# Retention branch: the gate takes the group norm's weight and offset when it is evicted, the norm becomes two operations per head, and POOL does no arithmetic

## The chip, the cores and the metric

The kernel runs on one core of a Trainium2 chip. The metric is the device time of one execution in microseconds (us), the median of several runs. The engines are named as the profile names them: PE (TensorE matmuls), PEld (its weight loads), DVE (VectorE), ACT (ScalarE), POOL (GpSimd), SP (SyncE, which here only issues transfers).

## The reference

One layer of a hybrid decoder: from `h = rms_norm(x)` a wide projection gives an attention branch and a retention branch; both are merged through sigmoid gates, projected back, and followed by a squared-ReLU MLP. 256 positions, model width 2048, 8 retention heads with values of width 256. The part that matters here:

```
rg, rv ...   = h @ w_in                         # gate and values of the retention branch, 2048 columns each
y_ret        = retention_chunkwise(rq, rk, rv)  # (256, 8 heads, 256)
mu, var      = mean and variance of y over the 256 columns of a head
yn           = (y - mu) * rsqrt(var + 1e-6)
o_ret        = silu(rg) * (yn * ret_gn_g + ret_gn_b)
merged       = sigmoid(ga) * (o_attn @ w_up_attn) + sigmoid(gb) * (o_ret @ w_up_ret)
```

## The kernel before

All large products run as three fp32r matmuls of a high and a low part (lines 335 to 337: high x high, high x low, low x high), 128 rows by 512 columns each. Weights are streamed in tiles; ACT copies half a tile into its high part `whi` (line 293), DVE subtracts to get the low part `wlo` (line 294). One such half tile, called a split below, serves two steps of the inner dimension k, that is 12 matmuls. `whi` and `wlo` have three buffers each, so a split is made while the two before it are still to be multiplied.

`run_block` (line 319) multiplies one block of 512 output columns: 16 steps of k, for two row tiles t = 0, 1. In each step it first calls `step()`, which advances every piece of side work in the list `work` by one `yield`; side work is written as generators, and this sets where its instructions stand among the matmuls. `drain()` runs what is left. Within what the program order allows, the compiler's scheduler may still place the instructions of one engine in another order.

The retention part is the loop at line 695, over j = 0..3, two heads at a time. Each round multiplies the gate block RG (512 columns), evicts it as silu (ACT's sigmoid in line 398, DVE's multiplication in line 707), multiplies the value block RV and evicts it. The side work `decayed` (lines 632 to 643) runs during RV of the same round. `retain` and `normed` (lines 645 to 693) run during the next block: RG of round j + 1, or the block GB after the last round. So `normed` of round 0 stands in RG of round 1, and so on.

In `normed`, DVE takes means and variances (lines 677, 678), then a reciprocal square root in eleven tiny operations (lines 346 to 351), then (y - mu) * r in line 688. POOL multiplies by the weight (line 690), adds the offset (line 691) and multiplies by the gate (line 692), 512 columns each, for t = 0 and then t = 1. Seven steps of k after each was issued, PE transposes the result (line 368, a helper). The transposes of t = 0 stand before step 14 of the block and those of t = 1 before step 15, the last one. PE takes its instructions in order, so a transpose that waits holds back all matmuls behind it.

The tiles `mid` come from a ring of 11 buffers. Before, a round takes 6 of them: weight and offset `gb[0]`, `gb[1]` (loaded over POOL's queue, line 699), two gates, two value tiles.

Of the kernel before, what the change touches and what calls it, by code (L numbers as in the profile page):

```python
# [14 lines left out]
ALU = mybir.AluOpType  # L15
AX = mybir.AxisListType

P = 128
# [4 lines left out]
BN = 512  # L23
# [7 lines left out]
RV = 256  # L31
# [106 lines left out]
def block_kernel(ctx, tc, cst, rot, xt, gains, w, x, ret_gn_g, ret_gn_b, out):  # L138
    nc = tc.nc
# [21 lines left out]
    def nm(s):  # L161
        uid[0] += 1
        return f"{s}_{uid[0]}"

    def stage(shape=(P, BN)):
        return sp.tile(list(shape), F32, tag="stg", name=nm("stg"), bufs=n_stg)

    def mid(shape):
        return ep.tile(list(shape), F32, tag="mid", name=nm("mid"), bufs=n_mid)

    def small(w):
        return sp.tile([P, w], F32, tag="small", name=nm("small"), bufs=n_sm)
# [4 lines left out]
    def psum_a():  # L177
        return pa.tile([P, BN], F32, tag="pa", name=nm("pa"))
# [5 lines left out]
    work = []  # L184
# [6 lines left out]
    def drain():  # L191
        while work:
            step()
# [125 lines left out]
    def run_block(key, act, before=None):  # L319
        nk, n = B[key]  # L320
        ps = [pm.tile([P, BN], F32, tag="pm", name=nm("pm")) for _ in range(T)]
        for k in range(nk):
            if k % HC == 0:
                ws = weights((key, k // KC, k % KC // HC))
            if before:
                before(k)
            step()
            products(ps, [p[:, :n] for p in (ws[0][:, k % HC], ws[1][:, k % HC])], [act(k, t) for t in range(T)], k == 0, k == nk - 1)
        return [p[:, :n] for p in ps]
# [9 lines left out]
    def of(a):  # L339
        return lambda k, t: tuple(z[:, k, t * P:(t + 1) * P] for z in a[:2])  # L340


    def rsqrt(v, n, mul):

        a, y, u = small(n), small(n), small(n)
        nc.vector.tensor_scalar(a, v, mul, EPS, op0=ALU.mult, op1=ALU.add)
        nc.vector.tensor_scalar(y.bitcast(I32), a.bitcast(I32), -0.5, float(0x5F3759DF), op0=ALU.mult, op1=ALU.add)
        for _ in range(3):
            nc.vector.tensor_tensor(u, y, y, op=ALU.mult)
            nc.vector.scalar_tensor_tensor(u, u, -0.5, a, op0=ALU.mult, op1=ALU.mult)  # L350
            nc.vector.scalar_tensor_tensor(y, u, 1.5, y, op0=ALU.add, op1=ALU.mult)
        return y
# [9 lines left out]
    def transpose_in(act, k0, t, src, wait=2):  # L362

        for _ in range(wait):
            yield
        ps = psum_t()
        for c in range(4):
            nc.tensor.transpose(ps[:, c * P:(c + 1) * P], src[:, c * P:(c + 1) * P], ident)  # L368
        split_into(act, k0, 4, t, ps)
# [27 lines left out]
    def evict(dst, ps, t, func=AF.Copy):  # L397
        nc.scalar.activation(dst, ps, func, scale=r1[:, t:t + 1])
# [233 lines left out]
    def decayed(j, am):  # L632
        h0 = 2 * j
        yield
        psA = psum_a()
        for a in range(2):
            for t in range(T):
                nc.tensor.matmul(psA[:, (2 * a + t) * P:(2 * a + t + 1) * P], rkT[:, h0 + a, t * P:(t + 1) * P],
                                 rqT[:, h0 + a, t * P:(t + 1) * P], start=True, stop=True)
        for a in range(2):  # L640
            nc.vector.tensor_tensor(am[:, a * S:(a + 1) * S].rearrange("p (t i) -> p t i", t=T),
                                    psA[:, a * S:(a + 1) * S].rearrange("p (t i) -> p t i", t=T),
                                    dec[:, h0 + a].unsqueeze(1).to_broadcast([P, T, P]), op=ALU.mult)

    def retain(j, silu, rv, gb, am):
        h0 = 2 * j
        psR = psum_a()
        for a in range(2):
            nc.tensor.matmul(psR[:, a * RV:(a + 1) * RV], kz[:, h0 + a, :], rv[0][:, a * RV:(a + 1) * RV], start=True, stop=True)
        R = stage()  # L650
        nc.scalar.activation(R, psR, AF.Copy)
        yield
        ys = []
        for t in range(T):
            psy = psum_a()
            for a in range(2):
                nc.tensor.matmul(psy[:, a * RV:(a + 1) * RV], am[:, (2 * a + t) * P:(2 * a + t + 1) * P],
                                 rv[t][:, a * RV:(a + 1) * RV], start=True, stop=True)
            y = stage()
            nc.scalar.activation(y, psy, AF.Copy)  # L660
            ys.append(y)
            yield
        psc = psum_a()
        for a in range(2):
            nc.tensor.matmul(psc[:, a * RV:(a + 1) * RV], rqT[:, h0 + a, P:S], R[:, a * RV:(a + 1) * RV], start=True, stop=True)
        for a in range(2):
            y = ys[1][:, a * RV:(a + 1) * RV]
            nc.vector.scalar_tensor_tensor(y, psc[:, a * RV:(a + 1) * RV], xi[:, h0 + a:h0 + a + 1], y,
                                           op0=ALU.mult, op1=ALU.add)
        yield from normed(j, ys, silu, gb)  # L670

    def normed(j, ys, silu, gb):
        mv, vr = small(4 * T), small(2 * T)
        for t in range(T):
            for a in range(2):
                st = small(6)
                nc.vector.bn_stats(st, ys[t][:, a * RV:(a + 1) * RV])
                nc.vector.bn_aggr(mv[:, 4 * t + 2 * a:4 * t + 2 * a + 2], st)
        nc.vector.tensor_copy(vr, mv.rearrange("p (a b) -> p a b", b=2)[:, :, 1])
        yield  # L680
        r = rsqrt(vr, 2 * T, 1.0)
        yield
        for t in range(T):
            y = ys[t]
            for a in range(2):
                yy = y[:, a * RV:(a + 1) * RV]
                i = 2 * t + a
                nc.vector.tensor_scalar(yy, yy, mv[:, 2 * i:2 * i + 1], r[:, i:i + 1], op0=ALU.subtract, op1=ALU.mult)
            yield
            nc.gpsimd.tensor_tensor(y, y, gb[0], op=ALU.mult)  # L690
            nc.gpsimd.tensor_tensor(y, y, gb[1], op=ALU.add)  # L691
            nc.gpsimd.tensor_tensor(y, y, silu[t], op=ALU.mult)  # L692
            work.append(transpose_in(rT, 4 * j, t, y, W_GN))

    for j in range(4):
        gb = []
        for src in (ret_gn_g, ret_gn_b):
            g = mid([P, BN])
            nc.gpsimd.dma_start(g, src[:, j * BN:(j + 1) * BN].to_broadcast([P, BN]))
            gb.append(g)  # L700
        ps = run_block(("RG", j), of(hT))
        drain()
        silu = []
        for t in range(T):
            s = mid([P, BN])
            evict(s, ps[t], t, AF.Sigmoid)
            nc.vector.scalar_tensor_tensor(s, ps[t], r1[:, t:t + 1], s, op0=ALU.mult, op1=ALU.mult)
            silu.append(s)
        am = stage()
        work.append(decayed(j, am))  # L710
        ps = run_block(("RV", j), of(hT))
        rv = []
        for t in range(T):
            v = mid([P, BN])
            evict(v, ps[t], t)
            rv.append(v)
        work.append(retain(j, silu, rv, gb, am))


    for i in range(4):  # L720
# [122 lines left out]
    ys = {}  # L843
# [126 lines left out]
```

## Time and profile before

| | before |
|---|---|
| median of 3 runs | 1651.04 us (1648.32 to 1652.44) |
| the profiled execution, its own time | 1649.92 us |
| its span, first to last instruction | 1648.1 us |
| PE busy | 1632.5 us (99%) |
| DVE busy | 1155.4 us (70%) |
| ACT busy | 931.4 us (57%) |
| POOL busy | 103.1 us (6%) |
| mean granted clock of TensorE | 0.999 |

Times in the profile are counted from the start of the span. A matmul's bar overlaps the next one's, because matmuls are pipelined: a 128x512 matmul is shown with 0.39 us, and the next one starts 0.23 us after it.

### The profile page before, as it was taken

The page shows a single profiled execution, that of the slowest core. Times are in us where ns is not written, and L with a number is a line of the kernel's source. Part 1 is how long each engine was busy: PE and PEld are TensorE (multiplying, and loading weights), DVE is VectorE, ACT ScalarE, POOL GpSimd, SP SyncE. Part 2 cuts the span into 40 slices and gives each one's busy share as a digit, 9 for nine tenths or more (in the row PEclk, how much of TensorE's full clock was granted, in tenths as well). Part 3 has the DMA queues.
Part 4 walks back from the last instruction along what each step waited for, and adds up shares of the span by engine and source line. Part 5 has one row for each costly group of instructions (what it writes and reads, how often), then busy time and mean ns, then how long its engine had stood idle before and what let it go on. Part 6 is the DMA issues. An engine that isn't in the chain of part 4 may idle for free.

```text
span 1648.1 us, 19358 instructions
## 1 busy us (share of the span) xinstructions
PE 1632.5 (99%) x7466; PEld 1351.6 (82%) x7466; DVE 1155.4 (70%) x1316; ACT 931.4 (57%) x1150; POOL 103.1 (6%) x92
## 2 busy tenths in 40 slices
PE   9999999999999999999999999999999999999998
PEld 8977888888888778778888888888888888888887
DVE  6577776644554666564555578898989898989874
ACT  7556564444334444434444476676767676767672
POOL 0000000000000330220000000000000000000000
PEclk9999999999999999999999999999999999999999
DMA  9644445555555444445557655777777777767763
GB/s 346 223 144 176 148 149 187 181 191 192 199 186 197 157 171 167 175 171 187 194 188 266 209 209 209 230 230 230 230 229 230 228 228 218 230 221 228 229 196 136
DMA packets 62940, 334.47 MB, mean 203 GB/s; under 512 B 6656, under 2 KB 13184, under 8 KB 27264
## 3 DMA queue, kind: packets, MB, share of 16 engines
q1 hardware_dynamic: 51264, 309.62, 52.3%
q0 software_dynamic: 8704, 16.78, 6.8%
q10 hardware_dynamic: 2880, 6.83, 1.1%
q8 instruction: 58, 0.95, 0.2%
q14 instruction: 34, 0.28, 0.0%
HBM read 314.34 MB, written 18.87 MB: 202 GB/s over the span
## 4 chain that ended last, share of the span: by engine, by line
PE 56%; issue 3%; POOL 1%; DVE 0%; POOLq 0%
PE pf L335 7%; PE pf L337 7%; PE pf L336 7%; PE pm L337 6%; PE pm L335 6%; PE pm L336 6%; PE pq L337 5%; PE pq L335 5%; PE pq L336 5%; PE pt L368 1%; POOL stg L690 0%; PE pt L770 0%; POOL stg L691 0%; POOL stg L692 0%; DVE stg L885 0%
## 5 line engine op out<-in xcount | busy, mean ns | idle before, releaser
L294 DVE TENSOR_TENSOR wlo<-raw,whi 128x1024 fp32r<-128x1024 f32 (+2 forms) x564 | 678.3, 1211 | 411.1 <-ACT whi L293 405.8
L293 ACT ACTIVATE whi<-raw 128x1024 fp32r<-128x1024 f32 (+2 forms) x564 | 581.9, 1037 | 552.3 <-PE pm L337 433.6
L335 PE MATMUL pm<-whi,act 128*128 128x512 f32 (+1 forms) x1312 | 517.3, 395 | 1.7 <-ACT whi L293 1.7
L336 PE MATMUL pm<-wlo,act 128*128 128x512 f32 (+1 forms) x1312 | 507.5, 387 | 0.0
L337 PE MATMUL pm<-whi,act 128*128 128x512 f32 (+1 forms) x1312 | 506.8, 386 | 0.0
L335 PEld LDWEIGHTS pm<-whi,act 128*128 128x128 f32 x1312 | 246.9, 188 | 50.9 <-issue 3.2
L336 PEld LDWEIGHTS pm<-wlo,act 128*128 128x128 f32 x1312 | 247.1, 188 | 48.2 <-issue 1.9
L337 PEld LDWEIGHTS pm<-whi,act 128*128 128x128 f32 x1312 | 246.8, 188 | 47.6
L335 PE MATMUL pf<-whi,act 128*128 128x512 f32 x512 | 200.3, 392 | 0.0
L336 PE MATMUL pf<-wlo,act 128*128 128x512 f32 x512 | 199.6, 390 | 0.0
L337 PE MATMUL pf<-whi,act 128*128 128x512 f32 x512 | 199.6, 390 | 0.0
L294 DVE TENSOR_TENSOR wlo<-rawc,whi 128x1024 fp32r<-128x1024 f32 x112 | 136.8, 1221 | 26.8 <-ACT whi L293 25.6
L335 PE MATMUL pq<-whi,xf 128*128 128x512 f32 x392 | 154.5, 394 | 0.0
L337 PE MATMUL pq<-whi,xf 128*128 128x512 f32 x392 | 152.9, 390 | 0.0
L336 PE MATMUL pq<-wlo,xf 128*128 128x512 f32 x392 | 152.8, 390 | 0.0
L293 ACT ACTIVATE whi<-rawc 128x1024 fp32r<-128x1024 f32 x112 | 118.7, 1059 | 47.3 <-PE pf L337 23.3
L286 DVE TENSOR_TENSOR raw<-raw,raw 128x2048 f32<-128x2048 f32 x56 | 128.0, 2286 | 0.5
L337 PEld LDWEIGHTS pf<-whi,act 128*128 128x128 f32 x512 | 96.1, 188 | 20.0
L335 PEld LDWEIGHTS pf<-whi,act 128*128 128x128 f32 x512 | 96.1, 188 | 20.0 <-ACT whi L293 0.4
L336 PEld LDWEIGHTS pf<-wlo,act 128*128 128x128 f32 x512 | 96.2, 188 | 19.8
L882 POOL DMA_DIRECT2D sums<-ev x56 | 49.1, 966 | 833.0 <-ACT ev L881 832.5
L337 PEld LDWEIGHTS pq<-whi,xf 128*128 128x128 f32 x392 | 73.6, 188 | 15.4
(146 smaller groups left out, 1024.0 us busy)
## 6 DMA issues: line engine op xcount, KB each, us to landing
raw<-in_w_dram SPq DMA_DIRECT2D x220, 1024.0 KB, 4.8
rawc<-in_w_dram SPq DMA_DIRECT2D x56, 1024.0 KB, 6.2
sums<-ev POOLq DMA_DIRECT2D x56, 256.0 KB, 5.5
raw<-in_w_dram SPq DMA_DIRECT2D x12, 736.0 KB, 7.2
raw<-in_w_dram SPq DMA_DIRECT2D x7, 512.0 KB, 7.8
stg<-in_x_dram SPq DMA_DIRECT2D x8, 256.0 KB, 9.1
x<-in_x_dram ACTq DMA_DIRECT2D x2, 1024.0 KB, 7.5
sums<-x ACTq DMA_DIRECT2D x8, 256.0 KB, 2.4
```

The lines of the kernel that those rows point to most:

```text
L286: nc.vector.tensor_tensor(one, one, two, op=ALU.add)
L293: nc.scalar.activation(a, src, AF.Copy)
L294: nc.vector.tensor_tensor(b, src, a.bitcast(F32), op=ALU.subtract)
L335: nc.tensor.matmul(d, h, hi, start=first, stop=False, skip_group_check=skip)
L336: nc.tensor.matmul(d, h, lo, start=False, stop=False, skip_group_check=skip)
L337: nc.tensor.matmul(d, l, hi, start=False, stop=last, skip_group_check=skip)
L368: nc.tensor.transpose(ps[:, c * P:(c + 1) * P], src[:, c * P:(c + 1) * P], ident)
L882: nc.gpsimd.dma_start(sums[:, t, i * BN:(i + 1) * BN], z, accum_op=ALU.add)
```

## The change

The weight and offset leave `normed`. When the gate is evicted, DVE makes `s` = silu, then `u` = s * offset (line 708 of the changed kernel), then `s` = s * weight (line 709). `normed` then does per head and row tile ((y - mu) * s) in line 688 and (y * r + u) in line 690, both on DVE, 256 columns each. POOL keeps only the loads. A round now takes 8 `mid` buffers of the ring.

```
-                nc.vector.tensor_scalar(yy, yy, mv[:, 2 * i:2 * i + 1], r[:, i:i + 1], op0=ALU.subtract, op1=ALU.mult)
-            yield
-            nc.gpsimd.tensor_tensor(y, y, gb[0], op=ALU.mult)
-            nc.gpsimd.tensor_tensor(y, y, gb[1], op=ALU.add)
-            nc.gpsimd.tensor_tensor(y, y, silu[t], op=ALU.mult)
+                nc.vector.scalar_tensor_tensor(y[:, c], y[:, c], mv[:, 2 * i:2 * i + 1], sg[t][:, c],
+                                               op0=ALU.subtract, op1=ALU.mult)
+                nc.vector.scalar_tensor_tensor(y[:, c], y[:, c], r[:, i:i + 1], sb[t][:, c], op0=ALU.mult, op1=ALU.add)
+            yield
             work.append(transpose_in(rT, 4 * j, t, y, W_GN))
...
         for t in range(T):
-            s = mid([P, BN])
+            s, u = mid([P, BN]), mid([P, BN])
             evict(s, ps[t], t, AF.Sigmoid)
             nc.vector.scalar_tensor_tensor(s, ps[t], r1[:, t:t + 1], s, op0=ALU.mult, op1=ALU.mult)
-            silu.append(s)
+            nc.vector.tensor_tensor(u, s, gb[1], op=ALU.mult)
+            nc.vector.tensor_tensor(s, s, gb[0], op=ALU.mult)
+            sg.append(s)
+            sb.append(u)
```

The order of PE's instructions is the same before and after. Two places on DVE change, and one on ACT. First DVE at the end of a gate block (round 0 is shown; `mid` with the pm tile is the silu, L294 is the low part of the third split of the RV block, L641 is `decayed`). Before:

```order
L707 SCALAR_TENSOR_TENSOR mid_4099<-pm_3961,r_492,mid_4099 128x512
L707 SCALAR_TENSOR_TENSOR mid_4102<-pm_3962,r_492,mid_4102 128x512
L294 TENSOR_TENSOR wlo_4111<-raw_3997,whi_4110 128x1024
L641 TENSOR_TENSOR stg_4105<-pa_4120,dec 128x256 x2
L294 TENSOR_TENSOR wlo_4134<-raw_3997,whi_4133 128x1024
```

The same place in the changed kernel:

```order
L707 SCALAR_TENSOR_TENSOR mid_4099<-pm_3961,r_492,mid_4099 128x512
L708 TENSOR_TENSOR mid_4100<-mid_4099,mid_3959 128x512
L294 TENSOR_TENSOR wlo_4117<-raw_3997,whi_4116 128x1024
L709 TENSOR_TENSOR mid_4099<-mid_4099,mid_3957 128x512
L707 SCALAR_TENSOR_TENSOR mid_4105<-pm_3962,r_492,mid_4105 128x512
L641 TENSOR_TENSOR stg_4111<-pa_4126,dec 128x256
L708 TENSOR_TENSOR mid_4106<-mid_4105,mid_3959 128x512
L641 TENSOR_TENSOR stg_4111<-pa_4126,dec 128x256
L709 TENSOR_TENSOR mid_4105<-mid_4105,mid_3957 128x512
L294 TENSOR_TENSOR wlo_4140<-raw_3997,whi_4139 128x1024
```

The third split's low part now stands behind one added multiplication, the fourth split's low part (the last row) behind four.

Second, DVE at the end of `normed` (round 0, in RG of round 1; stg_4281 and stg_4296 are the y of t = 0 and t = 1, L350 and L351 the last of the reciprocal square root, L294 the low parts of splits). Before:

```order
L350 SCALAR_TENSOR_TENSOR small_4338<-small_4338,small_4336 128x4
L351 SCALAR_TENSOR_TENSOR small_4337<-small_4338,small_4337 128x4
L688 TENSOR_SCALAR stg_4281<-stg_4281,small_4309,small_4337 128x256 x2
L294 TENSOR_TENSOR wlo_4365<-raw_4183,whi_4364 128x1024
L688 TENSOR_SCALAR stg_4296<-stg_4296,small_4309,small_4337 128x256 x2
L294 TENSOR_TENSOR wlo_4391<-raw_4217,whi_4390 128x1024
```

The changed kernel, where stg_4287 and stg_4302 are these y, and `normed`'s first operation (L688, (y - mu) * s) stands further ahead, behind the means, as it needs no r:

```order
L294 TENSOR_TENSOR wlo_4373<-raw_4189,whi_4372 128x1024
L350 SCALAR_TENSOR_TENSOR small_4344<-small_4344,small_4342 128x4
L351 SCALAR_TENSOR_TENSOR small_4343<-small_4344,small_4343 128x4
L690 SCALAR_TENSOR_TENSOR stg_4287<-stg_4287,small_4343,mid_4100 128x256
L690 SCALAR_TENSOR_TENSOR stg_4287<-stg_4287,small_4343,mid_4100 128x256
L690 SCALAR_TENSOR_TENSOR stg_4302<-stg_4302,small_4343,mid_4106 128x256 x2
L294 TENSOR_TENSOR wlo_4395<-raw_4223,whi_4394 128x1024
```

Behind the last L690 the y of both row tiles are complete and nothing of POOL follows; one split's low part moved ahead of them.

On ACT, at the end of a gate block, the high part of RV's third split moves from behind both sigmoids to between them; nothing else changes its place there.

## Rows read from the trace of the kernel before

**Rows 1.** The page, parts 1 and 2.

```profile
PE 1632.5 (99%) x7466; PEld 1351.6 (82%) x7466; DVE 1155.4 (70%) x1316; ACT 931.4 (57%) x1150; POOL 103.1 (6%) x92
...
PE   9999999999999999999999999999999999999998
...
PEclk9999999999999999999999999999999999999999
```

**Rows 2.** Waits of PE: total us, times, longest.

```profile
PE pt L368 <- POOL stg L692: 8.2, 4, 2.1
```

**Rows 3.** Timeline, end of RG in round 1: start us, us, engine, instruction.

```profile
560.28 0.39 PE L337 MATMUL pm<-whi,act 128*128 128x512 f32 x1
560.51 0.60 PE L368 MATMUL pt<-csb,stg 128*128 128x128 f32 x4
...
562.11 0.39 PE L337 MATMUL pm<-whi,act 128*128 128x512 f32 x1
562.35 2.12 POOL L692 TENSOR_TENSOR stg<-stg,mid 128x512 f32<-128x512 f32 x1
...
564.53 0.84 PE L368 MATMUL pt<-csb,stg 128*128 128x128 f32 x4 [2.04 <-POOL stg L692]
```

**Rows 4.** Timeline, the same transposes in the three later rounds.

```profile
617.45 0.66 PE L368 MATMUL pt<-csb,stg 128*128 128x128 f32 x4 [2.02 <-POOL stg L692]
...
668.87 0.66 PE L368 MATMUL pt<-csb,stg 128*128 128x128 f32 x4 [2.06 <-POOL stg L692]
...
720.29 0.66 PE L368 MATMUL pt<-csb,stg 128*128 128x128 f32 x4 [2.06 <-POOL stg L692]
```

**Rows 5.** Timeline of DVE, ACT, POOL in `normed` of round 0.

```profile
550.97 0.74 DVE L688 TENSOR_SCALAR stg<-stg,small,small 128x256 f32<-128x256 f32 x2
...
551.85 2.15 POOL L690 TENSOR_TENSOR stg<-stg,mid 128x512 f32<-128x512 f32 x1 [302.36 <-DVE stg L688]
...
552.76 2.75 DVE L688 TENSOR_SCALAR stg<-stg,small,small 128x256 f32<-128x256 f32 x2
...
555.27 1.06 ACT L293 ACTIVATE whi<-raw 128x1024 fp32r<-128x1024 f32 x1 [1.66 <-PE pm L337]
...
556.57 2.31 DVE L294 TENSOR_TENSOR wlo<-raw,whi 128x1024 fp32r<-128x1024 f32 x1
```

**Rows 6.** Stretches (length, busy us by engine, then PEclk), and the next L638.

```profile
564.00:568.00 4.00, 3.47 (x11) 2.90 (x12) 1.28 (x2) 1.31 (x3) 1.53 (x3) 0.61 0.85 291
...
569.37 1.05 PE L638 MATMUL pa<-rqT,rk 128*128 128x128 f32 x8
...
620.70 1.06 PE L638 MATMUL pa<-rqT,rk 128*128 128x128 f32 x8
```

**Rows 7.** Single lines: duration ns min/median/max, first and last start.

```profile
L733 DVE TENSOR_TENSOR mg<-mg,sgb x8: 681/684/687, 810.1 to 878.7; 128x512 f32<-128x512 f32 x8
...
L486 DVE SCALAR_TENSOR_TENSOR mid<-stg,iw,mid x30: 342/414/486, 91.9 to 113.5; 128x128 f32<-128x128 f32 x15, 128x256 f32<-128x256 f32 x15
...
L641 DVE TENSOR_TENSOR stg<-pa,dec x8: 412/417/421, 518.1 to 674.1; 128x256 f32<-128x256 f32 x8
```

**Rows 8.** Timeline, gate eviction of round 2 and the first splits of RV.

```profile
618.89 1.38 ACT L398 ACTIVATE mid<-pm,r 128x512 f32<-128x512 f32 x2
...
619.61 1.45 DVE L707 SCALAR_TENSOR_TENSOR mid<-pm,r,mid 128x512 f32<-128x512 f32 x2
...
621.25 1.23 DVE L294 TENSOR_TENSOR wlo<-raw,whi 128x1024 fp32r<-128x1024 f32 x1 [0.20 <-ACT whi L293]
...
625.92 0.39 PE L336 MATMUL pm<-wlo,act 128*128 128x512 f32 x1
...
628.64 0.39 PE L336 MATMUL pm<-wlo,act 128*128 128x512 f32 x1
```

**Rows 9.** Stretch of 30 us around `normed` of round 0: busy us PE, PEld, DVE, ACT, POOL.

```profile
541.00:571.00 30.00, 27.96 (x125) 22.96 (x124) 22.75 (x39) 11.92 (x14) 13.37 (x8) 0.94 0.48 167
```

**Rows 10.** Timeline of POOL: the load for round 2.

```profile
564.43 0.56 POOL L699 DMA_DIRECT2D mid<-in_ret_gn_g_dram  x1
```

More of the change, by code (lines that the diff above doesn't have):

```diff
@@ L643, in decayed, with retain @@
                                     dec[:, h0 + a].unsqueeze(1).to_broadcast([P, T, P]), op=ALU.mult)
-    def retain(j, silu, rv, gb, am):
+    def retain(j, sg, rv, sb, am):
         h0 = 2 * j
@@ L669, in retain, with normed @@
                                            op0=ALU.mult, op1=ALU.add)
-        yield from normed(j, ys, silu, gb)
-    def normed(j, ys, silu, gb):
+        yield from normed(j, ys, sg, sb)
+    def normed(j, ys, sg, sb):
         mv, vr = small(4 * T), small(2 * T)
@@ L685, in normed @@
             for a in range(2):
-                yy = y[:, a * RV:(a + 1) * RV]
+                c = slice(a * RV, (a + 1) * RV)
                 i = 2 * t + a
-                nc.vector.tensor_scalar(yy, yy, mv[:, 2 * i:2 * i + 1], r[:, i:i + 1], op0=ALU.subtract, op1=ALU.mult)
+                nc.vector.scalar_tensor_tensor(y[:, c], y[:, c], mv[:, 2 * i:2 * i + 1], sg[t][:, c],
+                                               op0=ALU.subtract, op1=ALU.mult)
+                nc.vector.scalar_tensor_tensor(y[:, c], y[:, c], r[:, i:i + 1], sb[t][:, c], op0=ALU.mult, op1=ALU.add)
             yield
-            nc.gpsimd.tensor_tensor(y, y, gb[0], op=ALU.mult)
-            nc.gpsimd.tensor_tensor(y, y, gb[1], op=ALU.add)
-            nc.gpsimd.tensor_tensor(y, y, silu[t], op=ALU.mult)
             work.append(transpose_in(rT, 4 * j, t, y, W_GN))
@@ L702, in block_kernel @@
         drain()
-        silu = []
+        sg, sb = [], []
         for t in range(T):
-            s = mid([P, BN])
+            s, u = mid([P, BN]), mid([P, BN])
             evict(s, ps[t], t, AF.Sigmoid)
             nc.vector.scalar_tensor_tensor(s, ps[t], r1[:, t:t + 1], s, op0=ALU.mult, op1=ALU.mult)
-            silu.append(s)
+            nc.vector.tensor_tensor(u, s, gb[1], op=ALU.mult)
+            nc.vector.tensor_tensor(s, s, gb[0], op=ALU.mult)
+            sg.append(s)
+            sb.append(u)
         am = stage()
@@ L716, in block_kernel @@
             rv.append(v)
-        work.append(retain(j, silu, rv, gb, am))
+        work.append(retain(j, sg, rv, sb, am))
     for i in range(4):
```

## The prediction

> **What bounds the kernel now.** The page comes first: PE is busy for 1632.5 of 1648.1 us, and the granted clock reads full in every slice [rows 1]. So the change can only win what PE does not use or uses at a lower clock, 15.6 us plus clock losses, and any work on DVE or POOL counts only where PE waits for it. The waits of PE come second: the retention branch has one entry, the transposes of line 368 waiting for POOL's line 692, four times, 8.2 us [rows 2]. The timeline shows which they are: in the block after each round, the transposes of t = 0 start on time, 0.23 us after the matmul ahead of them, but those of t = 1 find POOL still in its last multiplication [rows 3], and so in all four rounds [rows 4]. The reader should see POOL's rate there: six operations of about 2.2 us, one after the other, from 551.85 to 564.47, behind a DVE that was through with t = 0 at 551.7 [rows 3, 5].
>
> **What goes away.** First, the four waits. The printed idle times are 2.04, 2.02, 2.06 and 2.06 us [rows 3, 4], together 8.18. They are counted from the end of the matmul ahead (562.11 + 0.39 + rounding), while an undisturbed transpose starts 0.16 us before that end (560.51 against 560.28 + 0.39). So each wait costs 0.16 more: 8.18 + 0.64 = 8.8 us. The restart adds a little: a bar of four transposes is 0.60 long undisturbed and 0.66 after a wait [rows 3, 4], 0.06 x 4 = 0.2.
>
> Second, a fall of the clock. After the first wait the granted clock is 0.61 on average from 564 to 568 us [rows 6], that is a stretch at 1.2 instead of 2.4 GHz; PE had stood idle just before. From the late transposes to L638 of the next block there are the same instructions in every round: 569.37 - 564.53 = 4.84 us with the fall [rows 3, 6], 620.70 - 617.45 = 3.25 us without [rows 4, 6]. The fall costs 1.6 us. It followed one of four nearly equal waits.
>
> The Trainium skill ("TensorE: Matmul & The Clock Gate", Part 1) says that the gate halves the clock when PE has been idle, and that its watch runs free of the kernel, so that the same program can meet it at another phase. The trace agrees as far as it goes: equal waits, one fall. By that rule the gain from falls would be anything from none to four times 1.6 us, in other executions; the sum takes the one that the trace shows.
>
> Sum of what goes: 8.8 + 0.2 + 1.6 = 10.6 us.
>
> **What is added on DVE, and what hides it.** The trace has the prices nearly exactly. A multiplication of 128x512 in SBUF takes 0.68 us (line 733). A scalar_tensor_tensor with SBUF sources is bounded by line 486, whose 128x128 and 128x256 forms lie between 0.34 and 0.49 [rows 7]; I take 0.49 for 256 columns, the upper end. A round adds 4 x 0.68 = 2.7 at the gate and 8 x 0.49 = 3.9 in the norm, and loses four tensor_scalar, 1.5 at their undisturbed 0.74 a pair [rows 5]: 5.2 us more on DVE. Two pieces come back: the second pair took 2.75 instead of 0.74 while POOL ran, and a low part took 2.31 [rows 5] against 1.23 [rows 8]; that alone is 3.1 us a round. So DVE gains almost no load; what matters is whether the splits queued behind the new work are late for PE.
>
> *At the gate.* In round 2 DVE begins with line 707 at 619.61 [rows 8]. By the new order the low part of RV's third split is ready at 619.61 + 0.75 + 0.68 + 1.23 = 622.3; PE reads it first at 625.92 [rows 8], 3.6 us later. Its high part, 1.06 on ACT [rows 5] behind one sigmoid of 0.69 [rows 8], starts no later than now. The fourth split's low part ends behind two 707, four multiplications, the third split and two of line 641 at 0.42 [rows 7]: 619.61 + 1.5 + 2.7 + 1.2 + 0.8 + 1.2 = 627.1; PE reads it at 628.64 [rows 8]. That is 1.5 us to spare. I cost it at nothing; without this cover each round would pay what exceeds it.
>
> *In the norm.* DVE had its r at 550.97 [rows 5]. In front of the last L690 now stand four hoisted operations (2.0), one split (1.2) and four L690 (2.0), so y is complete at 556.1 at the latest. PE wants it at 560.51 (t = 0) and at 562.11 + 0.23 = 562.34 (t = 1) [rows 3]: more than 4 us early. The next low part then ends at 557.3. A split is wanted 24 matmuls or 5.4 us after its high part starts, plus one matmul for the low part; the high parts start at 555.27 [rows 5] and one split (12 x 0.227 = 2.7) before, so this one is wanted at 558.2, and the one after, done at 558.6, at 560.9. Before, that latter one was done at 556.57 + 2.31 = 558.9 [rows 5], and PE did not wait for it.
>
> *Loads and buffers.* Weight and offset are now wanted at the gate, a block sooner. Those of round 2 were issued at 564.43 [rows 10], behind POOL's arithmetic, and are wanted at about 620 [rows 8]: some 55 us of cover. With 8 of 11 buffers a round, the load takes the buffers of the second u and the first value tile of the round before last, both read by then. The value tiles take buffers of the gate products of the round before, which the norm has read a block earlier. Cost: nothing.
>
> In all slices behind the retention part PE is at work to the end [rows 1], so a shift moves everything after it rigidly. The sum stays at -10.6 us: 1649.9 - 10.6 = 1639.3 for the profiled execution. That execution lies 1.1 us below the median, so against the median I forecast 1651.0 - 10.6 = **1640.4 us**.
>
> **Rivals.** *More or fewer falls of the clock.* If the execution behind the median had no fall, 9.0 us go: 1642.0. If it had three, 13.8 go: 1637.2. The rows show one in four waits and no more.
>
> *A small new wait at the gate.* If PE waits up to 1 us at each of the four gates, 4 us come back: 1644.4. For it speaks the thin spare of 1.5 us there; against it, that all prices are rows of the same shape.
>
> *The wait only moves.* If the fourth split is late by as much as the transposes are now (2.2 us), nothing is won: about 1651. That wants 1.5 + 2.2 = 3.7 us more in four multiplications, 0.68 + 0.93 = 1.6 us each, against 0.684 in eight rows out of eight [rows 7].
>
> *DVE is full and pays for everything.* Then each added us on DVE is an us on PE: 4 x 5.2 = 20.8 us, less 10.6, gives 1661.2. It decides from the point where DVE has no idle time around the norm. The row shows 22.75 of 30 us busy, part of it slowed by POOL [rows 9].
>
> The Trainium skill ("Perfetto Trace Analysis", Optimizing Scalar/DVE Operations) speaks for this rival: where DVE is saturated, moving work to ScalarE or even GpSimd may pay, and the change does the reverse. The same section warns that the two share a read port, so that such a move may not help; the 2.75 us pair bears that out.
>
> **How the numbers follow.** All four waits go, nothing new, one fall: 0.62. More falls or none: 0.15. Small new wait: 0.12. The wait only moves: 0.07. DVE full: 0.04. The likeliest gives 1640.4. A range from 1637.0 to 1645.5 takes in the first three cases and leaves out 0.11 and an edge. About 0.3% (5 us) is what a measurement of this kernel can tell from no change. The first three lie beyond it (6.6 us at least): faster 0.89. The fourth is the same: 0.07. The fifth is slower: 0.04.
>
> **What would show it.** In the changed profile PE's waits should have no entry at line 368 for retention, the transposes of t = 1 should start 0.23 us after the matmul ahead of them, the clock should not fall around 565 us, and low parts during the norm should take 1.2 us. Lines 708 and 709 should show 0.68, lines 688 and 690 at most 0.49. The prediction is wrong if PE's line 336 waits for `wlo` in the first eight steps of RV, if the transposes wait for DVE's line 690, or if ACT's evictions are late because the gate's tiles come free later.

## The result, and the profile after

The changed kernel takes 1640.03 us (median of 4 runs, 1639.73 to 1640.34) against 1651.05 us before (4 runs). The ratio is 0.9935, 95% interval 0.9918 to 0.9952. The forecast was 1640.4 us, in a range from 1637.0 to 1645.5.

The page of the changed kernel, its head and part 1, answers to [rows 1]:

```profile
span 1638.5 us, 19348 instructions
...
PE 1630.5 (100%) x7466; PEld 1350.0 (82%) x7466; DVE 1153.9 (70%) x1348; ACT 931.7 (57%) x1150; POOL 53.2 (3%) x68
```

POOL lost half its busy time, yet DVE, which took the work over, did not gain any: 1153.9 us against 1155.4. PE has 8 us idle left instead of 15.6.

The waits of PE in the changed kernel (total us, times, longest), beside [rows 2]:

```profile
PE pm L335 <- ACT whi L293: 2.3, 2, 1.2
PE pa L212 <- DVE warm L209: 1.1, 1, 1.1
PE pt L424 <- DVE stg L418: 0.3, 1, 0.3
```

The entry of line 368 is gone and none came for it. What is left stands ahead of the retention part. The timeline of the changed kernel at the places of [rows 3, 4] shows the transposes of t = 1 in the four rounds, for round 0 with those of t = 0 and the matmul ahead:

```profile
561.50 0.60 PE L368 MATMUL pt<-csb,stg 128*128 128x128 f32 x4
...
563.09 0.39 PE L337 MATMUL pm<-whi,act 128*128 128x512 f32 x1
...
563.32 0.60 PE L368 MATMUL pt<-csb,stg 128*128 128x128 f32 x4
...
612.39 0.60 PE L368 MATMUL pt<-csb,stg 128*128 128x128 f32 x4
...
661.45 0.60 PE L368 MATMUL pt<-csb,stg 128*128 128x128 f32 x4
...
710.52 0.60 PE L368 MATMUL pt<-csb,stg 128*128 128x128 f32 x4
```

No row carries a wait in brackets, each bar is 0.60 long, and 563.32 - 563.09 = 0.23 us. From the transposes of t = 0 in round 0 to those of t = 1 in round 3 it is 710.52 - 561.50 = 149.0 us; before it was 720.29 - 560.51 = 159.8 [rows 3, 4]. So 10.8 us went inside the retention part, all that the medians show (11.0) but 0.2. The two spans differ by less, 9.6 us, since the profiled execution of the change reached the retention part 1.0 us later (561.50 against 560.51); the kernel before did so too in another execution, shown below.

The stretch in which the clock fell [rows 6], and the 30 us around the norm [rows 9], in the changed kernel (length, busy us of PE, PEld, DVE, ACT, POOL, then the granted clock):

```profile
564.00:568.00 4.00, 4.00 (x23) 3.47 (x22) 3.87 (x7) 2.87 (x4) 0.00 (x0) 1.00 0.73 252
541.00:571.00 30.00, 30.00 (x142) 25.07 (x141) 23.71 (x49) 13.06 (x16) 1.07 (x2) 1.00 0.51 179
```

The granted clock stays at 1.00, that is 2.4 GHz, PE is busy throughout, and DVE went from 22.75 to 23.71 us of 30.

### The profile page after: what moved, and what is told of

Same layout as the page of the kernel before. It is cut to its first block, busy times and chain, and to the rows that moved or that the text cites. A ratio compares the mean times of both kernels' runs of the same rounds, so it can differ in the third digit from the quotient of the medians.

```text
span 1638.5 us, 19348 instructions
## 1 busy us (share of the span) xinstructions
PE 1630.5 (100%) x7466; PEld 1350.0 (82%) x7466; DVE 1153.9 (70%) x1348; ACT 931.7 (57%) x1150; POOL 53.2 (3%) x68
## 4 chain that ended last, share of the span: by engine, by line
PE 99%; DVE 0%; DMA 0%; ACT 0%; SPq 0%; issue 0%
PE pm L335 19%; PE pm L336 19%; PE pm L337 18%; PE pf L335 7%; PE pf L337 7%; PE pf L336 7%; PE pq L337 5%; PE pq L335 5%; PE pq L336 5%; PE pt L368 1%; PE pa L564 1%; PE pa L537 1%; PE pa L467 0%; PE pa L657 0%; DMA raw<-in_w_dram 0%; PE pt L556 0%
## 5 line engine op out<-in xcount | busy, mean ns | idle before, releaser
L294 DVE TENSOR_TENSOR wlo<-raw,whi 128x1024 fp32r<-128x1024 f32 (+2 forms) x564 | 669.3, 1195 | 412.3 <-ACT whi L293 406.9
L294 DVE TENSOR_TENSOR wlo<-rawc,whi 128x1024 fp32r<-128x1024 f32 x112 | 136.6, 1220 | 26.4 <-ACT whi L293 25.2
L336 PEld LDWEIGHTS pq<-wlo,xf 128*128 128x128 f32 x392 | 73.7, 188 | 14.8
```

The costliest lines, as they stand in the source:

```text
L294: nc.vector.tensor_tensor(b, src, a.bitcast(F32), op=ALU.subtract)
L336: nc.tensor.matmul(d, h, lo, start=False, stop=False, skip_group_check=skip)
```

## Experiments

The theory: PE paid only because the transposes of t = 1 stood ahead of POOL's end, four waits and a fall of the clock. The rivals: POOL's arithmetic costs by slowing DVE beside it; or DVE, now fuller, pays elsewhere.

**e1: the kernel before, with its transposes later.** POOL's arithmetic stays. The transposes wait eleven steps instead of seven, and what then is left of the side work runs into the next block.

```
-    W_NORM, W_SOFT, W_GN = 3, 5, 7
+    W_NORM, W_SOFT, W_GN = 3, 5, 11
...
         ps = run_block(("RG", j), of(hT))
-        drain()
...
         ps = run_block(("GB", i), of(hT))
-        if i == 0:
+        if i == 1:
             drain()
+        if i == 0:
             sgb = px.tile([P, T, D], F32, tag="big2", name="sgb")
```

> The kernel before, with POOL's arithmetic untouched, but the transposes stand four steps of k (5.4 us) later, in the block behind. Theory (PE paid only because the transposes of t = 1 stood 2.2 us ahead of POOL's end): no wait of PE for line 692, no fall of the clock there, 1651.0 - 10.6 = 1640.4 us, about 0.994 of before. Rival (POOL's arithmetic costs by slowing DVE at the same time, and that is what the change took away): nothing is gained, 1651 us, 1.000.

Measured: 1640.26 us, ratio 0.9936 (0.9921 to 0.9951), the theory's number. In its timeline POOL's last operation of round 0, then both transposes, now in RV:

```profile
562.70 2.16 POOL L692 TENSOR_TENSOR stg<-stg,mid 128x512 f32<-128x512 f32 x1
...
567.24 0.60 PE L368 MATMUL pt<-csb,stg 128*128 128x128 f32 x4
569.06 0.60 PE L368 MATMUL pt<-csb,stg 128*128 128x128 f32 x4
```

POOL ends at 564.9, as slow as ever, and the transposes come after it. Low parts still take up to 2.31 us beside POOL, as before. The whole gain of the change is had without moving one operation off POOL, so the slowing of DVE cost nothing.

**e2: two POOL operations in the norm instead of three.** The changed kernel with this edit:

```
-                nc.vector.scalar_tensor_tensor(y[:, c], y[:, c], mv[:, 2 * i:2 * i + 1], sg[t][:, c],
-                                               op0=ALU.subtract, op1=ALU.mult)
-                nc.vector.scalar_tensor_tensor(y[:, c], y[:, c], r[:, i:i + 1], sb[t][:, c], op0=ALU.mult, op1=ALU.add)
-            yield
+                nc.vector.tensor_scalar(y[:, c], y[:, c], mv[:, 2 * i:2 * i + 1], r[:, i:i + 1], op0=ALU.subtract, op1=ALU.mult)
+            yield
+            nc.gpsimd.tensor_tensor(y, y, sg[t], op=ALU.mult)
+            nc.gpsimd.tensor_tensor(y, y, sb[t], op=ALU.add)
```

> The changed kernel, but the norm is split again: DVE does (y - mu) * r, POOL multiplies by s and adds u, two operations for each row tile instead of three. Theory: POOL's chain of four operations at 2.2 us ends at about 551.9 + 8.8 = 560.7 in the count of before, ahead of 562.3 where PE wants t = 1; no wait, 1640.4 us, 0.994. Rival (slowing of DVE by POOL): two thirds of POOL's operations stay, so at most a third of the gain, 1647.5 us, 0.998.

Measured: 1639.87 us, ratio 0.9935 (0.992 to 0.995). The timeline, POOL's last operation of round 0 and the transposes of t = 1:

```profile
558.20 2.15 POOL L691 TENSOR_TENSOR stg<-stg,mid 128x512 f32<-128x512 f32 x1
...
562.66 0.60 PE L368 MATMUL pt<-csb,stg 128*128 128x128 f32 x4
```

POOL is done at 560.35, 2.3 us early. It needed to lose only one operation of three; the second edit of the change, the norm in two operations on DVE, adds nothing to that.

**e3: the gate products on POOL.** The changed kernel with lines 708 and 709 moved:

```
-            nc.vector.tensor_tensor(u, s, gb[1], op=ALU.mult)
-            nc.vector.tensor_tensor(s, s, gb[0], op=ALU.mult)
+            nc.gpsimd.tensor_tensor(u, s, gb[1], op=ALU.mult)
+            nc.gpsimd.tensor_tensor(s, s, gb[0], op=ALU.mult)
```

> The changed kernel, but POOL makes the two gate products (lines 708 and 709), four operations at 2.2 us = 8.8 us in each round, at the start of RV; they are wanted in the next block, 20 us later. Theory: POOL's work costs nothing where nobody waits; 1640.0 us, ratio to before 0.9935, and the low parts beside it take about 2.3 instead of 1.2 us without a wait of PE. Rival (slowing of DVE by POOL): the low parts of RV's first splits come late, PE waits for wlo 1 us or more in each round, 1644 us or more.

Measured: 1640.2 us, ratio 0.9935 (0.9919 to 0.9952). Its timeline at the gate of round 0, POOL and two splits on DVE:

```profile
517.17 1.27 POOL L708 TENSOR_TENSOR mid<-mid,mid 128x512 f32<-128x512 f32 x1 [295.17 <-DVE mid L707]
...
517.34 2.19 DVE L294 TENSOR_TENSOR wlo<-raw,whi 128x1024 fp32r<-128x1024 f32 x1 [0.30 <-ACT whi L293]
...
518.53 2.17 POOL L709 TENSOR_TENSOR mid<-mid,mid 128x512 f32<-128x512 f32 x1
...
520.98 2.04 DVE L294 TENSOR_TENSOR wlo<-raw,whi 128x1024 fp32r<-128x1024 f32 x1
```

The low parts are slowed as expected, and PE has no wait for them. POOL's work is free where nobody waits for its end.

**e4: the kernel before again.** No edit; one more profiled execution.

> The kernel before, unchanged, in another profiled execution. Theory: the four waits are the same, 2.0 us each; the number of falls of the clock behind them may differ (none to four), and the span follows it by 1.6 us each. Rival (the fall is a fixed part of this program): one fall, behind the first wait, span within 0.5 us of 1648.

Measured: 1650.94 us, span 1649.2. Its waits of PE:

```profile
PE pt L368 <- POOL stg L692: 8.2, 4, 2.1
```

Its timeline at the transposes of t = 0 and t = 1 in round 0:

```profile
561.46 0.60 PE L368 MATMUL pt<-csb,stg 128*128 128x128 f32 x4
565.47 0.66 PE L368 MATMUL pt<-csb,stg 128*128 128x128 f32 x4 [2.04 <-POOL stg L692]
```

Its stretch behind that wait (columns as above):

```profile
566.00:570.00 4.00, 4.00 (x13) 3.14 (x12) 2.19 (x3) 2.78 (x4) 0.47 (x1) 0.57 0.90 340
```

The same four waits, and one fall (0.57), behind the first. By its letter this is the rival's forecast for the number of falls and not for the span, which is 1.1 us longer than in [rows 3]'s execution because PE reached the retention part 1.0 us later. Two executions don't tell whether the place is fixed. The number of falls is not fixed. In the stretch above the clock lost (1 - 0.57) x 4.00 = 1.7 us, which is 0.001 of the span, so an execution whose mean clock is listed as 1.000 has no room for such a fall. The mean clocks of the 22 runs of before beside these experiments go from 0.998 to 1.000, and the three at 1.000 are the three fastest: 1649.31 us in a group with a median of 1650.87, 1648.67 and 1648.92 in one with 1650.68. They had none, and they lie 1.6 to 2.0 us below the medians, about the price of one. How many falls the other runs had, these means don't tell.

**e5: one more POOL operation for each row tile.** The kernel before with the offset added a second time (its output has the offset twice):

```
             nc.gpsimd.tensor_tensor(y, y, silu[t], op=ALU.mult)
+            nc.gpsimd.tensor_tensor(y, y, gb[1], op=ALU.add)
```

> The kernel before with one more POOL operation for each row tile (the offset is added a second time). Theory: POOL's chain for t = 1 ends 4.4 us later, so each of the four waits of PE grows by 4.4 us: 1650.9 + 17.6 = 1668.5, and up to three more falls of the clock at 1.6 us each, 1673.3 at most; ratio 1.011 to 1.014. Rival (PE's waits in the trace are not what the time is made of, other slack takes them up): clearly less than 17 us.

Measured: 1667.6 us, ratio 1.0105 (1.0091 to 1.0119), 16.9 us more than before. Its waits of PE:

```profile
PE pt L368 <- POOL stg L693: 19.0, 4, 4.8
```

Its timeline, POOL's last two operations of round 0:

```profile
565.65 1.26 POOL L692 TENSOR_TENSOR stg<-stg,mid 128x512 f32<-128x512 f32 x1
566.99 1.26 POOL L693 TENSOR_TENSOR stg<-stg,mid 128x512 f32<-128x512 f32 x1
```

Its stretches during the first wait (first row, DVE is the third of the busy times) and behind the four waits:

```profile
565.00:569.00 4.00, 0.69 (x5) 0.70 (x6) 0.05 (x1) 0.00 (x0) 3.84 (x5) 0.96 0.74 262
...
568.00:572.00 4.00, 3.69 (x12) 3.02 (x13) 1.44 (x2) 1.62 (x3) 1.30 (x3) 0.59 0.52 183
...
622.00:626.00 4.00, 2.10 (x7) 1.90 (x8) 0.31 (x1) 0.60 (x1) 2.81 (x4) 0.67 0.68 262
...
677.00:685.00 8.00, 5.68 (x16) 4.68 (x17) 2.44 (x4) 2.92 (x4) 2.19 (x2) 0.57 0.29 116
...
736.00:760.00 24.00, 24.00 (x101) 19.85 (x102) 9.48 (x9) 10.35 (x11) 0.00 (x0) 0.93 0.38 133
```

The waits grew by 19.0 - 8.2 = 10.8 us, 2.7 each and not 4.4: once DVE has stopped for want of work (0.05 us busy of 4), POOL's operations take 1.26 instead of 2.2 us. Behind every wait the clock now falls, in the third round for twice as long (0.57 over 8 us). That is four falls' worth more than before's one; at 1.6 us each 6.4 us, and 10.8 + 6.4 = 17.2 against 16.9 measured. Waits and falls are what the time is made of. The total fell short of the forecast (1668.5 us) by little only because falls made up for waits that were smaller than counted; the size of the added wait was a miss.

**e6 and e7: more work on DVE at the gate.** The changed kernel with two (e6, shown) or four (e7, `range(4)`) more operations for each row tile, each the larger of `s` and itself:

```
             nc.vector.tensor_tensor(s, s, gb[0], op=ALU.mult)
+            for _ in range(2):
+                nc.vector.tensor_tensor(s, s, s, op=ALU.max)
```

> The changed kernel with four more DVE operations of 128x512 at each gate (the product with the weight is compared with itself and kept), all ahead of the fourth split's low part by the order. By the prediction's way of counting on the changed kernel's trace, that low part ends at 621.3 in round 2 and is wanted at 623.5, 2.2 us to spare; 2.7 us more leave PE waiting 0.5 us in each round: 2 us, 1642 us, 0.995. Rival (DVE is full and pays for everything): four rounds of 2.7 us, 1651 us, 1.000.

> The same with eight more, 5.5 us a round. Counted as above: 5.5 - 2.2 = 3.3 us of wait in each round, 13 us, and up to four falls of the clock at 1.6 us: 1653 to 1660 us, 1.001 to 1.005; PE waits for wlo at line 336. Rival (DVE full): 22 us, 1662 us. Rival (the side work finds idle time anyway): 1640 us.

Measured: e6 1640.74 us, ratio 0.9943 (0.9929 to 0.9956), 0.7 us above the change and not 2. e7 1653.3 us, ratio 1.0017 (1.0008 to 1.0026), 13.3 us above the change. That is the 13 us that were counted, but by luck: the waits came out smaller, and falls of the clock made up for it, as follows. First the timeline of the changed kernel itself at the gate of round 2, the fourth split's low part and PE reading it:

```profile
620.10 1.22 DVE L294 TENSOR_TENSOR wlo<-raw,whi 128x1024 fp32r<-128x1024 f32 x1
...
623.52 0.39 PE L336 MATMUL pm<-wlo,act 128*128 128x512 f32 x1
```

The waits of PE in e7:

```profile
PE pm L336 <- DVE wlo L294: 9.1, 4, 2.3
```

The timeline of e6 at the gate of round 2, four DVE operations in a row, added ones (L711) and the change's own, then PE's weight load for the fourth split's low part:

```profile
618.26 0.68 DVE L711 TENSOR_TENSOR mid<-mid 128x512 f32<-128x512 f32 x1
618.86 0.68 DVE L708 TENSOR_TENSOR mid<-mid,mid 128x512 f32<-128x512 f32 x1
619.47 0.68 DVE L711 TENSOR_TENSOR mid<-mid 128x512 f32<-128x512 f32 x1
620.07 0.68 DVE L709 TENSOR_TENSOR mid<-mid,mid 128x512 f32<-128x512 f32 x1
...
623.81 0.19 PEld L336 LDWEIGHTS pm<-wlo,act 128*128 128x128 f32 x1 [0.30 <-DVE wlo L294]
```

The change has 623.52 - 621.32 = 2.2 us to spare there. Four operations in a row start 0.60 apart, though each bar is 0.68 long. So e6 adds 2.4 us, 0.2 a round beyond the spare (four rounds: 0.8, measured 0.7), and its weight load is just late. e7 adds 4.8, 2.6 beyond the spare; its waits of 2.3 with the 0.16 of the prediction's way of counting are 2.5, not the 3.3 expected. The clock explains the rest: 4 x 2.5 = 10 us of waits and 13.3 measured leave 3.3, two falls at 1.6. Two stretches of e7, behind its first and its last wait, show less than the full clock:

```profile
527.00:533.00 6.00, 4.79 (x14) 3.81 (x15) 3.43 (x4) 0.78 (x1) 0.00 (x0) 0.72 0.63 227
...
680.00:690.00 10.00, 7.72 (x28) 5.91 (x27) 7.48 (x11) 2.54 (x3) 0.00 (x0) 0.83 0.44 150
```

None of the rivals holds: DVE's work is free up to the spare, and paid beyond it.

**e8: retain one step later.** The changed kernel, with the transposes where they were:

```
-    W_NORM, W_SOFT, W_GN = 3, 5, 7
+    W_NORM, W_SOFT, W_GN = 3, 5, 6
...
         h0 = 2 * j
+        yield
         psR = psum_a()
```

> The changed kernel with retain one step of k later and the transposes at the same place, so that the first matmul of retain (line 649 before) finds its value tile evicted; now its weight load waits 0.3 us in each round, 1.2 us in all. Theory: these waits go, about 1.2 us or less, 1638.8 to 1640 us, 0.9928 to 0.9935; the y stand 1.4 us nearer to their transposes, still 4 us early, at no cost. Rival: the norm is late for the transposes, 1640 us or more.

Measured: 1639.99 us, ratio 0.994 (0.9927 to 0.9954), runs from 1638.0 to 1641.67. The waits of retain's first weight load are gone from its trace, but the runs scatter by more than the 1.2 us in question. Inconclusive.

## Why the prediction was right

**The waits.** The term of 8.8 + 0.2 us is shown by three runs: in e1 the change's whole gain comes with the transposes moved out of POOL's way, in e2 with a shorter POOL chain, and in e5 a longer chain costs more. In the retention part 10.8 us went where the sum says 10.6. The transposes of t = 1 also tell the waits from the fall. From those of one round to those of the next, the kernel before took 668.87 - 617.45 = 51.42 us without a fall [rows 4], and 720.29 - 668.87 = 51.42; the changed kernel takes 661.45 - 612.39 = 49.06. So a wait with its restart cost 2.4 us, where the sum has 9.0 / 4 = 2.25; the small rest is open. The round with the fall took 617.45 - 564.53 = 52.92 us [rows 3, 4], 1.5 more.

One reading was off without harm: of POOL's "six operations of about 2.2 us", the addition for t = 0 took 1.28 us (row in the last section). The sum does not use it.

**The fall of the clock.** Its 1.6 us belong to the sum as far as the execution behind the median has one fall. Both profiled executions of before have one, the change has none, and three of the 22 runs of before had none either (e4), which is one of the prediction's rivals; that the median had one was likely but not sure. The Trainium skill ("TensorE: Matmul & The Clock Gate", Part 1) says that the gate's watch runs free of the kernel, so that the same program can meet it at another phase. The runs agree: equal waits drew one fall or a long one in e5, one or none in e7. In the two profiled executions of before, though, it was the first wait both times. What picks the wait is open.

**DVE at the gate, costed at nothing.** Right, with more to spare than worked out: 2.2 us instead of 1.5, since operations in a row overlap: multiplications start 0.60 us apart and not 0.68. e6 and e7 find the edge there.

**DVE in the norm, costed at nothing.** Right. The forms of the changed kernel by line (duration ns min/median/max, first and last start), beside [rows 7]:

```profile
L688 DVE SCALAR_TENSOR_TENSOR stg<-stg,small,mid x16: 467/474/485, 543.7 to 696.1; 128x256 f32<-128x256 f32 x16
...
L690 DVE SCALAR_TENSOR_TENSOR stg<-stg,small,mid x16: 475/480/485, 553.6 to 702.0; 128x256 f32<-128x256 f32 x16
...
L709 DVE TENSOR_TENSOR mid<-mid,mid x8: 678/682/683, 518.8 to 668.6; 128x512 f32<-128x512 f32 x8
```

Its timeline at the end of the norm in round 0:

```profile
553.62 1.68 DVE L690 SCALAR_TENSOR_TENSOR stg<-stg,small,mid 128x256 f32<-128x256 f32 x4
```

The prediction's prices were 0.49 and 0.68. y is complete at 555.3, that is 554.3 in the count of before, against "556.1 at the latest" and 561.50 wanted. DVE's load did not rise, where the prediction had 5.2 us a round added and at least 3.1 returned. The added operations overlap (the four of line 690 take 1.68 us together, not 4 x 0.48), and more came back than the two pieces counted: before, two more low parts beside POOL took longer than 1.2 us.

```profile
559.09 2.02 DVE L294 TENSOR_TENSOR wlo<-raw,whi 128x1024 fp32r<-128x1024 f32 x1 [0.21 <-ACT whi L293]
...
561.81 1.55 DVE L294 TENSOR_TENSOR wlo<-raw,whi 128x1024 fp32r<-128x1024 f32 x1 [0.69 <-ACT whi L293]
```

**Loads.** The load of the weight for round 2 now starts at 549.67, ahead of [rows 10], as it no longer stands behind POOL's arithmetic; the offset's follows 5 us later, when DVE has read the buffer:

```profile
549.67 0.54 POOL L698 DMA_DIRECT2D mid<-in_ret_gn_g_dram  x1 [298.43 <-DVE stg L688]
554.79 0.54 POOL L698 DMA_DIRECT2D mid<-in_ret_gn_b_dram  x1 [4.59 <-DVE stg L690]
```

They are wanted near 615 (line 708 starts at 615.23), so the cover of a whole round stands. The buffers were worked out otherwise: the prediction had the loads take those of the second `u` and of a value tile, while both waits name DVE's reads of gate products (lines 688 and 690). It cost nothing.

**The rivals.** The wait that only moves, and DVE paying for everything, did not come about: no wait of PE for `wlo` or line 690, and the full clock around 565 us. The small new wait at the gate is what e6 shows four operations further on.

## What to carry to other kernels

A chain on a slow engine costs only what its end lies behind the instruction that waits for it, and the falls of the clock that such a wait may draw. Read from the timeline how late it is (here 2.2 us of a 12.6 us chain); moving the waiting instruction, shortening the chain by one operation in three, or moving all of it were then worth the same (e1, e2 and the change: 1640.26, 1639.87 and 1640.03 us). Before loading another engine with the work, count its spare time at the next instruction that somebody waits for: here 2.2 us at the gate. Beyond it each us was paid in each of the four rounds, with falls of the clock on top once the wait was 2.3 us long (e7).

## What the runs showed that was not expected

POOL's price depends on DVE as DVE's on POOL, but it is not one price alone and another in company. A POOL multiplication or addition of 128x512 took 1.26 us when DVE had nothing to do (e5), and a low part on DVE took 1.22 us without POOL's arithmetic. In company, either engine could keep about its own time while the other took longer. In e3, line 708 on POOL took 1.27 us beside a low part of 2.19 us, and then line 709 took 2.17. In the kernel before, five of POOL's six operations for round 0 took 2.12 to 2.35 us, but the addition for t = 0 took 1.28, while DVE's pair beside it took 2.75 instead of 0.74 [rows 5]:

```profile
554.08 1.28 POOL L691 TENSOR_TENSOR stg<-stg,mid 128x512 f32<-128x512 f32 x1
```

The longer bars look like operations that take turns, each with the other's time in its own; no run tests that by itself. A chain that was counted at 2.2 us an operation shrinks once DVE stands still, and so e5's waits grew by 2.7 us where 4.4 were counted.

In the profiled executions, PE's waits of some 2.0 us drew a fall of the clock once in four times (the kernel before, both times), those of 2.3 us twice in four (e7), those of 4.8 us every time (e5). A fall costs about 1.6 us, nearly as much as the shortest of these waits.
